# Second feed-forward product of a hybrid decoder layer: seven block products over 1,024 tokens in place of the plain product

## The chip, the cores and the metric

The kernel runs on one core of one Trainium2 chip. The metric is the device time of one execution in microseconds (us); lower is better.

## The reference, cut to what matters

One decoder layer is computed for a prompt of 2,048 tokens and for eight single-token samples that share all weights. It has three mixing branches (a state-space model, trailing pooling, cross-attention to 256 memory tokens), then a gated feed-forward layer:

```python
x = x + rmsnorm(merged @ p['w_out'], p['g_mix_post'])
hf = rmsnorm(x, p['g_ffn_pre']) @ p['w_ffn_in']
f = (jax.nn.silu(hf[..., :D_FF]) * hf[..., D_FF:]) @ p['w_ffn_out']
x = x + rmsnorm(f, p['g_ffn_post'])
```

`D_MODEL` is 1,024 and `D_FF` is 2,816, so `w_ffn_out` is 2,816 x 1,024: 22 blocks of 128 rows by 8 blocks of 128 columns. All data is float32.

## The kernel before, in words

Every matrix product keeps float32 accuracy by splitting each operand into a high and a low part (`split`, L170 to L172: ScalarE copies the high part, VectorE or GpSimd subtracts it to get the low part) and doing three matmuls, high x high, high x low, low x high. Tokens lie along the free axis. The 2,048 prompt tokens are four quarters of 512 (`q` 0 to 3); the eight samples ride along with quarters 0 and 1, four each, which makes their width 516 (`fwidth`). Two quarters make a half (`SB`: quarters 0 and 1, quarters 2 and 3).

**Stages.** Up to about 1,690 us of the span come the branches and the out-projection, quarter by quarter. Then the first feed-forward product, half by half (`ffn_in`, L1309; its pool of buffers is called `half`); then the second (`ffn_out`, L1383; pool `down`), quarter by quarter.

**First feed-forward stage.** For each half, `left` (L1298) loads 28 operand tiles (seven sums by four row blocks) from DRAM (`d_S`) through the four `xr` buffers and splits them into the `S` tiles. The 22 iterations of `ffn_in` each do seven block products with them (a Strassen-Winograd scheme over two quarters and two halves of the 1,024 rows, with 7 products instead of 8), in 7 x 24 = 168 matmuls of 258 or 256 columns. Each iteration needs a pair of weight blocks: `w_pair` (L262) loads two 512 KB tiles into the `wr` buffers (L258), forms four sums on VectorE (L265 to L268) and splits. `prefetch` emits the pair of iteration i+1 at the start of iteration i. At its end the iteration stores the two results, one for each quarter, to `d_f` (L1368). Three times in each iteration `step()` runs the next piece of the background work; during the first half that is `second_scale` (1 piece) and `sums(1)` (16 pieces), which make the second half's `d_S`. What is left of it is run by `flush()` after the 22nd iteration.

**Second feed-forward stage.** For each quarter, `load_f` (L1371) loads 22 tiles of `d_f` through `xr` and splits them into the `f` tiles (52 buffers). `ffn_out` does, for each of 8 output blocks, 22 x 3 matmuls in two column blocks (258 or 256 columns). Weights come in 24 pieces for each pass, 120 in all, because the last quarter is done in two halves of 256 columns with the weights loaded twice. ScalarE takes the result out of PSUM, once squared and once times the gain; `finish` (L1407) normalises, adds the residual and stores.

**What sets the order.** The Python code allocates named buffers from rings: `xr` has 4 buffers, `wr` 4, `wh` and `wl` 4, `tmp` 7. A scheduler places the instructions on each engine's queue, and may move them far ahead of their place in the program when their data and buffers are there. All loads and stores are issued from the SP queue, in its order. The following lines are the parts the steps refer to most:

```python
BUFS = {"U": 5, "G": 2, "ops": 6, "h": 16, "br": 24, "acc": 8, "rb2": 1,
        "xr": 4, "tmp": 7, "rb": 1, "wr": 4, "wh": 4, "wl": 4, "wt": 2,
        "ev": 4, "S": 56, "f": 52, "z": 8}
def w_load(key):
    raw = slot("wr")
    nc.sync.dma_start(raw, I["w_all"][_WIDX[key]])
    return raw
def flush():
    step(1 << 30)
```

Of the kernel before, what the change touches and what calls it, by code (L numbers as in the profile page):

```python
# [29 lines left out]
NB = BW // P  # L30
DFF = 2816
NF = DFF // P
FCH = (8, 8, 6)
FOFF = (0, 8, 16)
SB = ((0, 1), (2, 3))
KH = KD // 2
HW_ = TQ + NS // 2
# [19 lines left out]
def _weight_plan():  # L57
    us = [("us", i) for i in range(4)]
    glu = [("gl", i) for i in range(2)]
    proj = [("uq", 0), ("uq", 1), ("KT",), ("V",), ("uq", 2), ("uq", 3)]  # L60
    proj += [("up", 3), ("up", 2), ("up", 1), ("pw",), ("up", 0)]

    def gates(b, ahead):
        r = []
        for j in range(KD):
            if j % 2 == 0:
                r.append(("ub", b, j // 2))
            r.append(("gt", b, j))
        return [r[1], r[2], r[0]] + r[3:] if ahead else r

    wo = [("wo", m) for m in range(KD)]
    fo = [("fo", c, m) for m in range(KD) for c in range(len(FCH))]
    seq = [("wk", h) for h in range(NH)] + [("wv", i) for i in range(4)] + us
    for q in range(NQ):
        seq += proj
        for i, b in enumerate(ORDER[q]):
            if b == 0:
                seq += glu
            seq += gates(b, i != 1)
        seq += wo + us if q + 1 < NQ else wo  # L80
    for sb in range(len(SB)):
        seq += [("f1", f) for f in range(NF)]
    for q in range(NQ):
        seq += fo
    seq += fo
    return seq


_SEQ = _weight_plan()
_STORED = [k for k in dict.fromkeys(_SEQ) if k[0] not in ("KT", "V", "f1")]  # L90
_STORED += [(k, f) for f in range(NF) for k in ("fa", "fb")]
_WIDX = {k: i for i, k in enumerate(_STORED)}


def _ncols(key):
    if key[0] == "pw":
        return NB * P
    if key[0] == "fo":
        return FCH[key[1]] * P
    return KD * P  # L100


# [26 lines left out]
def trunk(ctx, tc, nc, I, O):  # L129
# [8 lines left out]
    SIZE = {"tmp": 528, "ops": 512, "G": 512, "wr": 1024, "wh": 1024, "wl": 1024, "wt": 1024,  # L138
            "ev": HW_, "S": HW_, "f": HW_, "z": HW_}
    COMMON = ("xr", "tmp", "rb", "rb2", "wr", "wh", "wl")  # L140
    stage = [None]

# [21 lines left out]
    def dram(shape, name):  # L164
        return drp.tile(shape, F32, tag=name, name=name, bufs=1)
# [41 lines left out]
    d_rb2 = dram([NQ, P, W520], "d_rb2")  # L207
    d_S = dram([len(SB), 7, KH, P, HW_], "d_S")
    d_f = dram([NQ, NF, P, HW_], "d_f")

    background = []
    queue = {"last": None, "open": True}
# [64 lines left out]
    def w_emit(i):  # L277
        key = seq[i]
        if key[0] == "f1":
            wstate["buf"][i] = w_pair(key[1])  # L280
            return
        n = _ncols(key)
        raw = slot("wr")
        if key[0] == "KT":
            src = d_kt
        elif key[0] == "V":
            src = d_v
        else:
# [1082 lines left out]
    def load_f(q, n):  # L1371
        ft = []
        for f_ in range(NF):
            raw = slot("xr")
            nc.sync.dma_start(raw[:, :n], d_f[q, f_, :, :n])
            hi, lo = slot("f", F32R), slot("f", F32R)
            split(hi[:, :n], lo[:, :n], raw[:, :n])
            ft.append((hi, lo))
        return ft

    def ffn_out(ft, bl, z, st):
        sl = slice(bl[0][0], bl[-1][0] + bl[-1][1])
        for m in range(KD):  # L1383
            ps = [psum() for _ in bl]
            for c in range(len(FCH)):
                hi, lo = wget("fo", c, m)
                for j in range(FCH[c]):
                    i = FOFF[c] + j
                    ws = slice(j * P, (j + 1) * P)
                    ah, al = ft[i]  # L1390
                    for p_, (o, nn) in zip(ps, bl):
                        T.matmul(p_[:, :nn], lhsT=hi[:, ws], rhs=ah[:, o:o + nn], start=i == 0, stop=False)
                        T.matmul(p_[:, :nn], lhsT=hi[:, ws], rhs=al[:, o:o + nn], start=False, stop=False)
                    for p_, (o, nn) in zip(ps, bl):
                        T.matmul(p_[:, :nn], lhsT=lo[:, ws], rhs=ah[:, o:o + nn], start=False, stop=i == NF - 1)
            if len(z) <= m:
                z.append(slot("z"))
            sq = st if m == 0 else slot("tmp")
            for p_, (o, nn) in zip(ps, bl):
                zs = slice(o, o + nn)  # L1400
                S.activation(sq[:, zs], p_[:, :nn], AF.Square)
                S.activation(z[m][:, zs], p_[:, :nn], AF.Copy, scale=g_fpost[:, m:m + 1])
            if m > 0:
                V.tensor_tensor(st[:, sl], st[:, sl], sq[:, sl], ADD)
            step()

    def finish(q, z, st, bl):  # L1407
        sl = slice(bl[0][0], bl[-1][0] + bl[-1][1])
        if q + 1 == NQ:
            rb = spread(rsqrt_rows(st, bl), 0)[:, :sl.stop - sl.start]  # L1410
        else:
            rb = slot("rb")
            rsqrt_quick(rb, st, bl)
            rb = rb[:, sl]
        yield
        e = min(sl.stop, TQ)
        for k in range(KD):
            xt = slot("xr")
            load_half(xt, d_x2[:, k], q)
            zk = z[k][:, sl]  # L1420
            V.tensor_tensor(zk, zk, rb, MUL)
# [100 lines left out]
    stage[0] = down.__enter__()  # L1522
    slot("z")
    for q in range(NQ):
        n = fwidth(q)
        ft = load_f(q, n)
        z = []
        st = slot("tmp")
        for bl in ([[(0, n // 2), (n // 2, n // 2)]] if q + 1 < NQ else [[x] for x in HALVES]):
            ffn_out(ft, bl, z, st)  # L1530
            flush()
            background.append(finish(q, z, st, bl))
    flush()
    down.__exit__(None, None, None)

# [7 lines left out]
def _pack(a):  # L1543
# [8 lines left out]
    for key, i in _WIDX.items():  # L1552
# [11 lines left out]
        elif kind == "pw":  # L1564
            v = a["pool_w"][0].transpose(1, 0, 2).reshape(P, -1)
        elif kind == "gl":
            v = np.concatenate([kt(a["ssm_w_glu"][0][:, m * P:(m + 1) * P]) for m in (2 * key[1], 2 * key[1] + 1)], axis=1)
        elif kind == "ub":
            w = a["w_branch_up"][0][key[1]]
            v = np.concatenate([kt(w[:, m * P:(m + 1) * P]) for m in (2 * key[2], 2 * key[2] + 1)], axis=1)  # L1570
        elif kind == "gt":
            o = 3 * BW + key[1] * DM + key[2] * P
            v = kt(w_in[:, o:o + P])
        elif kind == "wo":
            v = kt(a["w_out"][0][:, key[1] * P:(key[1] + 1) * P])
        elif kind == "fa":
            v = kt(a["w_ffn_in"][0][:, key[1] * P:(key[1] + 1) * P])
        elif kind == "fb":
            v = kt(a["w_ffn_in"][0][:, DFF + key[1] * P:DFF + (key[1] + 1) * P])
        else:  # L1580
            o = FOFF[key[1]] * P
            v = kt(a["w_ffn_out"][0][o:o + FCH[key[1]] * P, key[2] * P:(key[2] + 1) * P])
# [51 lines left out]
```

## Time and profile before

| What | Value |
|---|---|
| Time, median of 3 runs (lowest to highest) | 3139.98 us (3139.03 to 3144.41) |
| The profiled execution's own time | 3146.45 us |
| Its span, first to last instruction | 3144.5 us |
| TensorE matmul busy, share of the span | 2996.9 us, 95% |
| VectorE busy | 1858.3 us, 59% |
| ScalarE busy | 1214.7 us, 39% |
| GpSimd busy | 741.6 us, 24% |
| First feed-forward stage, from its first matmul to its last | 1696.5 to 2598.3 us |
| Second feed-forward stage, from its first matmul to the end | 2599.9 to 3144.5 us |

TensorE is the engine that is nearly always at work, so a stage is read by how many matmuls it has, how long one takes when nothing holds it up, and where the count falls short. Busy time of TensorE overlaps itself (matmuls are pipelined), so counts over a window, and not busy shares, give the real rate.

### The profile page before, as it was taken

The page shows a single profiled execution, that of the slowest core. Times are in us where ns is not written, and L with a number is a line of the kernel's source. Part 1 is how long each engine was busy: PE and PEld are TensorE (multiplying, and loading weights), DVE is VectorE, ACT ScalarE, POOL GpSimd, SP SyncE. Part 2 cuts the span into 40 slices and gives each one's busy share as a digit, 9 for nine tenths or more (in the row PEclk, how much of TensorE's full clock was granted, in tenths as well). Part 3 has the DMA queues.
Part 4 walks back from the last instruction along what each step waited for, and adds up shares of the span by engine and source line. Part 5 has one row for each costly group of instructions (what it writes and reads, how often), then busy time and mean ns, then how long its engine had stood idle before and what let it go on. Part 6 is the DMA issues. An engine that isn't in the chain of part 4 may idle for free.

```text
span 3144.5 us, 51655 instructions
## 1 busy us (share of the span) xinstructions
PE 2996.9 (95%) x20479; PEld 2764.9 (88%) x20479; DVE 1858.3 (59%) x3187; ACT 1214.7 (39%) x2105; POOL 741.6 (24%) x630
## 2 busy tenths in 40 slices
PE   7989998799999999999996999999999999999997
PEld 6778877689997888878885999999999998999997
DVE  7777756664538644585566855557555554445364
ACT  4532434322445333452333433335333334334343
POOL 2565244532245122440222000000000000011012
PEclk8989999899999999999997999999999999999999
DMA  6344333662334433354364732225222225445475
GB/s 210 112 161 138 120 121 116 163 218 91 127 121 149 137 102 127 120 174 133 110 219 143 233 114 76 78 77 175 81 81 81 81 84 176 153 153 170 159 253 171
DMA packets 205730, 433.02 MB, mean 138 GB/s; under 512 B 47472, under 2 KB 55216, under 8 KB 205488
## 3 DMA queue, kind: packets, MB, share of 16 engines
q1 hardware_dynamic: 205488, 429.72, 43.1%
q8 instruction: 160, 2.62, 0.4%
q14 instruction: 82, 0.67, 0.1%
HBM read 362.82 MB, written 66.49 MB: 137 GB/s over the span
## 4 chain that ended last, share of the span: by engine, by line
PE 82%; DVE 5%; DMA 5%; issue 3%; POOL 2%; ACT 2%; SPq 1%; DVEq 0%; POOLq 0%; ACTq 0%
PE pa L117 78%; PE pb L117 3%; DMA xr<-d_f 1%; DVE wl L172 1%; PE pb L120 1%; DMA xr<-in_ck 1%; DMA xr<-d_S 1%; DVE acc L1238 1%; DMA xr<-in_cv_t 0%; ACT wh L171 0%; SPq L679 0%; DMA ops<-d_ops 0%; POOL acc L1239 0%; DMA xr<-d_qs 0%; DVE G L815 0%
## 5 line engine op out<-in xcount | busy, mean ns | idle before, releaser
L117 PE MATMUL pa<-S,wh 128*128 128x258 f32 (+1 forms) x4928 | 887.4, 283 | 26.1 <-ACT S L171 20.1
L171 ACT ACTIVATE wh<-wr 128x1024 fp32r<-128x1024 f32 (+1 forms) x460 | 458.2, 996 | 1022.4 <-PE pa L117 744.1
L117 PEld LDWEIGHTS pa<-S,wh 128*128 128x128 f32 x4928 | 762.5, 190 | 29.4 <-ACT S L171 21.4
L117 PE MATMUL pa<-S,wl 128*128 128x258 f32 (+1 forms) x2464 | 693.6, 282 | 0.3 <-DVE wl L172 0.3
L117 PE MATMUL pa<-h,wh 128*128 128x512 f32 (+2 forms) x2560 | 667.2, 356 | 19.5 <-ACT tmp L1037 7.4
L172 DVE TENSOR_TENSOR wl<-wr,wh 128x1024 fp32r<-128x1024 f32 x372 | 434.2, 1169 | 393.5 <-ACT wh L171 380.8
L117 PEld LDWEIGHTS pa<-h,wh 128*128 128x128 f32 x2560 | 438.4, 192 | 86.5 <-ACT tmp L1037 7.6
L117 PE MATMUL pa<-br,wh 128*128 128x512 f32 (+2 forms) x1848 | 471.3, 351 | 15.0 <-ACT wh L171 8.8
L117 PE MATMUL pa<-f,wh 128*128 128x258 f32 (+1 forms) x2816 | 468.9, 283 | 5.9 <-DVE f L172 3.0
L117 PEld LDWEIGHTS pa<-S,wl 128*128 128x128 f32 x2464 | 465.6, 189 | 0.5 <-DVE wl L172 0.5
L117 PE MATMUL pa<-h,wl 128*128 128x512 f32 (+2 forms) x1280 | 420.7, 355 | 0.0
L117 PEld LDWEIGHTS pa<-f,wh 128*128 128x128 f32 x2816 | 400.1, 190 | 8.4 <-DVE f L172 4.3
L117 PEld LDWEIGHTS pa<-br,wh 128*128 128x128 f32 x1848 | 311.6, 190 | 62.8 <-ACT wh L171 8.8
L172 POOL TENSOR_TENSOR wl<-wr,wh 128x1024 fp32r<-128x1024 f32 (+1 forms) x88 | 214.2, 2436 | 442.2 <-ACT wh L171 392.5
L117 PE MATMUL pa<-f,wl 128*128 128x258 f32 (+1 forms) x1408 | 312.3, 283 | 4.5 <-DVE wl L172 4.5
L117 PE MATMUL pa<-br,wl 128*128 128x512 f32 (+2 forms) x924 | 295.4, 350 | 1.0 <-DVE wl L172 1.0
L117 PEld LDWEIGHTS pa<-h,wl 128*128 128x128 f32 x1280 | 231.4, 192 | 33.6
L1365 POOL TENSOR_TENSOR tmp<-tmp,ev 128x516 f32<-128x516 f32 (+1 forms) x44 | 59.9, 1362 | 841.2 <-ACT tmp L1364 820.9
L172 DVE TENSOR_TENSOR wl<-wt,wh 128x1024 fp32r<-128x1024 f32 x88 | 108.1, 1228 | 223.5 <-ACT wh L171 223.5
L117 PEld LDWEIGHTS pa<-f,wl 128*128 128x128 f32 x1408 | 229.8, 189 | 4.7 <-DVE wl L172 4.7
L117 PEld LDWEIGHTS pa<-br,wl 128*128 128x128 f32 x924 | 164.1, 190 | 24.3 <-DVE wl L172 1.4
L1339 ACT ACTIVATE ev<-pa 128x258 f32<-128x258 f32 (+1 forms) x264 | 101.0, 385 | 196.7 <-PE pa L117 166.8
(329 smaller groups left out, 3486.7 us busy)
## 6 DMA issues: line engine op xcount, KB each, us to landing
wr<-in_w_all SPq DMA_DIRECT2D x408, 512.0 KB, 3.5
ops<-d_ops SPq DMA_DIRECT2D x112, 256.0 KB, 3.6
xr<-in_x_t SPq DMA_DIRECT2D x80, 256.0 KB, 3.7
xr<-d_x SPq DMA_DIRECT2D x72, 256.0 KB, 4.1
wr<-in_w_all SPq DMA_DIRECT2D x40, 384.0 KB, 3.4
d_f<-tmp SPq DMA_DIRECT2D x44, 258.0 KB, 4.7
xr<-d_f SPq DMA_DIRECT2D x44, 258.0 KB, 3.7
d_f<-tmp SPq DMA_DIRECT2D x44, 256.0 KB, 4.3
```

The lines of the kernel that those rows point to most:

```text
L117: self._done(self.nc.tensor.matmul(*a, **k))
L120: self._done(self.nc.tensor.transpose(*a, **k))
L171: S.activation(dst_hi, src, AF.Copy)
L172: (eng or V).tensor_tensor(dst_lo, src, f(dst_hi), SUB)
L1238: V.tensor_tensor(zk, zk, rb[:, :n], MUL)
L1339: both(lambda u, s: S.activation(dst[:, s], X[u][:, :w], AF.Copy))
L1365: G.tensor_tensor(f0[:, :n], f0[:, :n], p1[:, :n], MUL)
```

## The change

The second product becomes seven block products too, over a half (two quarters, 1,024 tokens) at a time: rows of `f` in two blocks of 11 x 128 (`KF` = 11), columns of `w_ffn_out` in two blocks of 4 x 128. Seven products (in the order `OUT_ORDER`), each 4 output blocks by 11 row blocks by 3 matmuls, replace the eight that the plain product would be.

- The left operand's four sums are made in the first stage by `out_sums`: for each of 11 row pairs, four loads of `d_f` into `xr`, four GpSimd operations, four stores to the new `d_fs`. `ffn_in` walks its 22 blocks in the order 0, 11, 1, 12, ... (`FORD`), and queues the pair before last as background work at every second iteration; the last pair is queued after the loop and run by `flush()`.
- The weights' four sums are made by `out_weights`, six background pieces queued behind `sums(1)` in the first half: for each, four 512 KB loads into `wr`, four GpSimd operations, four stores to the new `d_T`.
- In the second stage, `load_f` loads 11 tiles for each of the 14 products (one product ahead; 44 `f` buffers), from `d_f` or `d_fs`. Weights come in six pieces for each product; with the last product of the second half done in two halves of 256 columns, 90 pieces. The second half's other products use one column block of 512. VectorE adds each product to its running sums out of PSUM; ScalarE squares, GpSimd (VectorE at the very end) adds the squares.
- In the last `finish`, the residual tiles are loaded once into `z` buffers instead of twice into `xr`.

```diff
-            "ev": 4, "S": 56, "f": 52, "z": 8}
+            "ev": 4, "S": 56, "f": 44, "z": 16, "st": 3}
...
-        split(hi[:, :n], lo[:, :n], raw[:, :n], G if key[0] in ON_POOL or i >= len(seq) - KD else V)
+        split(hi[:, :n], lo[:, :n], raw[:, :n], G if key[0] in ON_POOL or i >= len(seq) - len(FPC) else V)
...
-        for f_ in range(NF):
+        for at, f_ in enumerate(FORD):
...
+            if at % 2 and at > 1:
+                background.append(out_sums(sb, at // 2 - 1))
             step()
+        background.append(out_sums(sb, KF - 1))
+
+    def out_sums(sb, j):
+        n = fwidth(SB[sb][0])
+        A = []
+        for q in SB[sb]:
+            for f_ in (j, j + KF):
+                t = slot("xr")
+                nc.sync.dma_start(t[:, :n], d_f[q, f_, :, :n])
+                A.append(t[:, :n])
+        a11, a12, a21, a22 = A
+        G.tensor_tensor(a22, a21, a22, ADD)
+        G.tensor_tensor(a21, a11, a21, SUB)
+        G.tensor_tensor(a11, a22, a11, SUB)
+        G.tensor_tensor(a12, a12, a11, SUB)
+        for i, t in enumerate((a22, a11, a21, a12)):
+            nc.sync.dma_start(d_fs[sb, i, j, :, :n], t)
+        yield
+
+    def out_weights():
+        for c in range(len(FPC)):
+            n = FPC[c] * P
+            b11, b12, b21, b22 = (w_load(("fo", r, m, c))[:, :n] for r in range(2) for m in range(2))
+            G.tensor_tensor(b22, b22, b12, SUB)
+            G.tensor_tensor(b12, b12, b11, SUB)
+            G.tensor_tensor(b11, b11, b22, ADD)
+            G.tensor_tensor(b21, b21, b11, SUB)
+            for i, t in enumerate((b21, b12, b11, b22)):
+                nc.sync.dma_start(d_T[i, c, :, :n], t)
+            yield
...
+        for m in range(KH):
             ps = [psum() for _ in bl]
+            for k in range(KF):
+                c, j = divmod(m * KF + k, 8)
+                if j == 0:
+                    wpiece[0] = wget("w2", i, c)
...
+            elif i == 1:
+                c11.append(slot("z"))
+                plus(c11[m], u[m], ps)
+                squares(0, c11[m])
...
+            for _ in range(3):
+                next(loader, None)
             step()
...
         if sb + 1 < len(SB):
             background.append(second_scale(NQ - 1))
             background.append(sums(sb + 1))
+            background.append(out_weights())
         ffn_in(sb, got)
         flush()
...
+    plan = [(sb, i) for sb in range(len(SB)) for i in OUT_ORDER]
+    ft = []
+    run(load_f(*plan[0], ft))
+    for at, (sb, i) in enumerate(plan):
...
+        loader = load_f(*plan[at + 1], nxt) if at + 1 < len(plan) else iter(())
+        for bl in out_halves(sb, i):
+            ffn_out(sb, i, ft, bl, C, st, loader)
```

## Rows read from the trace of the kernel before

**Rows 1.** The page: busy time of TensorE, and the chain that ended last.

```profile
PE 2996.9 (95%) x20479; PEld 2764.9 (88%) x20479; DVE 1858.3 (59%) x3187; ACT 1214.7 (39%) x2105; POOL 741.6 (24%) x630
...
PE 82%; DVE 5%; DMA 5%; issue 3%; POOL 2%; ACT 2%; SPq 1%; DVEq 0%; POOLq 0%; ACTq 0%
```

**Rows 2.** Stretches, with counts: window, length, PE, PEld, DVE, ACT, POOL, PEclk, DMA share, GB/s.

```profile
1690.00:1745.00 55.00, 38.85 (x257) 36.42 (x258) 46.58 (x79) 29.77 (x53) 6.93 (x5) 0.80 0.76 235
...
2165.00:2190.00 25.00, 24.28 (x197) 23.44 (x196) 19.68 (x33) 14.51 (x27) 1.30 (x1) 1.00 0.70 212
2190.00:2598.00 408.00, 408.00 (x3446) 408.00 (x3445) 219.56 (x367) 149.98 (x268) 27.16 (x21) 1.00 0.28 83
2598.00:2640.00 42.00, 36.23 (x266) 33.91 (x266) 26.07 (x37) 22.46 (x37) 0.00 (x0) 0.96 0.78 240
2640.00:3000.00 360.00, 360.00 (x3025) 360.00 (x3024) 156.29 (x202) 134.62 (x226) 24.82 (x16) 1.00 0.49 159
```

**Rows 3.** A stream of 512-column matmuls, earlier stage: start, us; 27 such `wl` rows.

```profile
1540.27 0.40 PE L117 MATMUL pa<-br,wl 128*128 128x512 f32 x1
...
1558.38 0.39 PE L117 MATMUL pa<-br,wl 128*128 128x512 f32 x1
```

**Rows 4.** SP queue, first feed-forward stage: weight loads of two iterations.

```profile
1901.61 0.33 SPq L258 DMA_DIRECT2D wr<-in_w_all  x1
...
1905.29 0.33 SPq L258 DMA_DIRECT2D wr<-in_w_all  x1
...
1921.70 0.47 SPq L258 DMA_DIRECT2D wr<-in_w_all  x1
```

**Rows 5.** SP queue, quarter 1: loads into the `xr` buffers.

```profile
506.56 0.43 SPq L382 DMA_DIRECT2D xr<-in_x_t  x1
...
556.43 0.37 SPq L1084 DMA_DIRECT2D xr<-d_qs  x1
556.86 0.97 SPq L1088 DMA_DIRECT2D xr<-in_ck  x2
...
696.65 0.63 SPq L382 DMA_DIRECT2D xr<-in_x_t  x1
```

**Rows 6.** Weight splits and GpSimd operations, 2300 to 3145 us: busy, mean ns, idle before.

```profile
L172 DVE TENSOR_TENSOR wl<-wr,wh 128x1024 fp32r<-128x1024 f32 x89 | 111.1, 1248 | 138.5 <-ACT wh L171 138.4
L171 ACT ACTIVATE wh<-wr 128x1024 fp32r<-128x1024 f32 x94 | 99.6, 1060 | 197.0 <-PE pa L117 183.5 <-DMA wr<-in_w_all 6.3 <-issue 4.6
...
L1365 POOL TENSOR_TENSOR tmp<-tmp,ev 128x512 f32<-128x512 f32 x15 | 19.4, 1293 | 277.7 <-ACT tmp L1364 277.7
...
L172 POOL TENSOR_TENSOR wl<-wr,wh 128x1024 fp32r<-128x1024 f32 x5 | 12.0, 2399 | 11.8 <-ACT wh L171 11.8
```

**Rows 7.** Time to landing: weight pairs (min/median/max), then stores and loads (median).

```profile
DMA to landing us min/median/max: 3.1/4.2/6.8
...
d_f<-tmp SPq DMA_DIRECT2D x44, 256.0 KB, 4.3
xr<-d_f SPq DMA_DIRECT2D x44, 256.0 KB, 4.2
```

**Rows 8.** The end of the first stage: last matmul, and the two last stores.

```profile
2598.05 0.28 PE L117 MATMUL pa<-S,wl 128*128 128x256 f32 x1
...
2600.02 0.33 SPq L1368 DMA_DIRECT2D d_f<-tmp  x1
...
2601.75 0.33 SPq L1368 DMA_DIRECT2D d_f<-tmp  x1
```

**Rows 9.** VectorE in the tail, waiting for residual tiles.

```profile
3138.32 0.43 DVE L1422 TENSOR_TENSOR z<-z,xr 128x256 f32<-128x256 f32 x1 [3.34 <-DMA xr<-d_x]
3141.43 0.43 DVE L1422 TENSOR_TENSOR z<-z,xr 128x256 f32<-128x256 f32 x1 [2.69 <-DMA xr<-d_x]
```

**Rows 10.** Two stretches in which GpSimd and VectorE are both busy.

```profile
2760.00:2770.00 10.00, 10.00 (x85) 10.00 (x85) 9.46 (x8) 2.95 (x6) 8.54 (x5) 1.00 0.46 145
3020.00:3030.00 10.00, 5.75 (x49) 5.54 (x48) 10.00 (x6) 4.80 (x8) 9.15 (x6) 1.00 0.57 180
```

More of the change, by code (lines that the diff above doesn't have):

```diff
@@ L32 @@
 NF = DFF // P
-FCH = (8, 8, 6)
-FOFF = (0, 8, 16)
+KF = NF // 2
+NPC = 4 * KF
+FPC = tuple(min(8, NPC - c) for c in range(0, NPC, 8))
+FORD = tuple(x for j in range(KF) for x in (j, j + KF))
+OUT_ORDER = (0, 1, 5, 4, 6, 2, 3)
+OUT_BLOCK = {0: (0, 0), 1: (1, 0), 2: (1, 1)}
+OUT_SUM = {4: 0, 5: 1, 6: 2, 2: 3}
 SB = ((0, 1), (2, 3))
@@ L81, in _weight_plan, with out_halves @@
     for sb in range(len(SB)):
[L82 to L85, printed above, removed]
-    return seq
+        seq += [("f1", f) for f in FORD]
+    for sb in range(len(SB)):
+        for i in OUT_ORDER:
+            seq += [("w2", i, c) for c in range(len(FPC))] * len(out_halves(sb, i))
+    return seq
+def out_halves(sb, i):
+    if sb == 0:
+        return [[(0, HW_ // 2), (HW_ // 2, HW_ // 2)]]
+    return [[(0, TQ // 2)], [(TQ // 2, TQ // 2)]] if i == OUT_ORDER[-1] else [[(0, TQ)]]
 _SEQ = _weight_plan()
-_STORED = [k for k in dict.fromkeys(_SEQ) if k[0] not in ("KT", "V", "f1")]
+_STORED = [k for k in dict.fromkeys(_SEQ) if k[0] not in ("KT", "V", "f1", "w2")]
 _STORED += [(k, f) for f in range(NF) for k in ("fa", "fb")]
+_STORED += [("fo", r, n, c) for c in range(len(FPC)) for r in range(2) for n in range(2)]
 _WIDX = {k: i for i, k in enumerate(_STORED)}
@@ L209, in trunk @@
     d_f = dram([NQ, NF, P, HW_], "d_f")
+    d_fs = dram([len(SB), 4, KF, P, HW_], "d_fs")
+    d_T = dram([4, len(FPC), P, KD * P], "d_T")
     background = []
@@ L287, in w_emit @@
             src = d_v
+        elif key[0] == "w2":
+            src = d_T[key[1] - 3, key[2]] if key[1] > 2 else I["w_all"][_WIDX[("fo",) + OUT_BLOCK[key[1]] + key[2:]]]
         else:
@@ L1374, in load_f @@
+    def load_f(sb, i, out):
+        n = fwidth(SB[sb][0])
+        for k in range(KF):
+            if i in OUT_SUM:
+                src = d_fs[sb, OUT_SUM[i], k]
+            else:
+                src = d_f[SB[sb][i // 2], k + KF * (i > 0)]
             raw = slot("xr")
-            nc.sync.dma_start(raw[:, :n], d_f[q, f_, :, :n])
+            nc.sync.dma_start(raw[:, :n], src[:, :n])
             hi, lo = slot("f", F32R), slot("f", F32R)
             split(hi[:, :n], lo[:, :n], raw[:, :n])
-            ft.append((hi, lo))
@@ L1379, in load_f, with ffn_out @@
-        return ft
-    def ffn_out(ft, bl, z, st):
+            out.append((hi, lo))
+            yield
+    def ffn_out(sb, i, ft, bl, C, st, loader):
+        u, c11, c12, c22 = C
         sl = slice(bl[0][0], bl[-1][0] + bl[-1][1])
-        for m in range(KD):
-            ps = [psum() for _ in bl]
[L1385 to L1404, printed above, removed]
@@ new lines, in plus, with squares @@
+        def plus(dst, src, ps):
+            for p_, (o, nn) in zip(ps, bl):
+                V.tensor_tensor(dst[:, o:o + nn], src[:, o:o + nn], p_[:, :nn], ADD)
+        def squares(row, t):
+            if st[row] is None:
+                st[row] = slot("st")
+                S.activation(st[row][:, :fwidth(SB[sb][0])], t[:, :fwidth(SB[sb][0])], AF.Square)
+                return
+            sq = slot("tmp")
+            S.activation(sq[:, sl], t[:, sl], AF.Square)
+            (G if sb == 0 or i != 3 else V).tensor_tensor(st[row][:, sl], st[row][:, sl], sq[:, sl], ADD)
@@ new lines, in ffn_out @@
+        for m in range(KH):
+            ps = [psum() for _ in bl]
+            for k in range(KF):
+                c, j = divmod(m * KF + k, 8)
+                if j == 0:
+                    wpiece[0] = wget("w2", i, c)
+                hi, lo = wpiece[0]
+                ws = slice(j * P, (j + 1) * P)
+                ah, al = ft[k]
+                for p_, (o, nn) in zip(ps, bl):
+                    T.matmul(p_[:, :nn], lhsT=hi[:, ws], rhs=ah[:, o:o + nn], start=k == 0, stop=False)
+                    T.matmul(p_[:, :nn], lhsT=hi[:, ws], rhs=al[:, o:o + nn], start=False, stop=False)
+                for p_, (o, nn) in zip(ps, bl):
+                    T.matmul(p_[:, :nn], lhsT=lo[:, ws], rhs=ah[:, o:o + nn], start=False, stop=k == KF - 1)
+            if i == 0:
+                u.append(slot("z"))
+                for p_, (o, nn) in zip(ps, bl):
+                    S.activation(u[m][:, o:o + nn], p_[:, :nn], AF.Copy)
+            elif i == 1:
+                c11.append(slot("z"))
+                plus(c11[m], u[m], ps)
+                squares(0, c11[m])
+            elif i == 5:
+                plus(u[m], u[m], ps)
+            elif i == 4:
+                c12.append(slot("z"))
+                plus(c12[m], u[m], ps)
+            elif i == 6:
+                c22.append(slot("z"))
+                plus(c22[m], c12[m], ps)
+                plus(u[m], u[m], ps)
+                squares(1, c22[m])
+            elif i == 2:
+                plus(c12[m], c12[m], ps)
+                squares(0, c12[m])
+            else:
+                plus(u[m], u[m], ps)
+                squares(1, u[m])
+            for _ in range(3):
+                next(loader, None)
@@ L1405, in ffn_out @@
             step()
+    wpiece = [None]
+    last_x = []
     def finish(q, z, st, bl):
@@ L1417, in finish @@
         for k in range(KD):
-            xt = slot("xr")
-            load_half(xt, d_x2[:, k], q)
+            if q + 1 < NQ:
+                xt = slot("xr")
+                load_half(xt, d_x2[:, k], q)
+            elif len(last_x) > k:
+                xt = last_x[k]
+            else:
+                xt = slot("z")
+                last_x.append(xt)
+                load_half(xt, d_x2[:, k], q)
             zk = z[k][:, sl]
-            V.tensor_tensor(zk, zk, rb, MUL)
+            V.scalar_tensor_tensor(zk, zk, g_fpost[:, k:k + 1], rb, MUL, MUL)
             (V if q + 1 == NQ and k % 2 else G).tensor_tensor(zk, zk, xt[:, sl], ADD)
@@ L1522, in trunk @@
     stage[0] = down.__enter__()
[L1523 to L1532, printed above, removed]
+    for tag in ("f", "z", "st"):
+        slot(tag)
+    plan = [(sb, i) for sb in range(len(SB)) for i in OUT_ORDER]
+    ft = []
+    run(load_f(*plan[0], ft))
+    for at, (sb, i) in enumerate(plan):
+        if i == OUT_ORDER[0]:
+            C, st = ([], [], [], []), [None, None]
+        nxt = []
+        loader = load_f(*plan[at + 1], nxt) if at + 1 < len(plan) else iter(())
+        for bl in out_halves(sb, i):
+            ffn_out(sb, i, ft, bl, C, st, loader)
+            if i == 2:
+                background.append(finish(SB[sb][0], C[1] + C[2], st[0], bl))
+            elif i == 3:
+                flush()
+                background.append(finish(SB[sb][1], C[0] + C[3], st[1], bl))
+        run(loader)
+        ft = nxt
     flush()
@@ L1580, in _pack @@
         else:
-            o = FOFF[key[1]] * P
-            v = kt(a["w_ffn_out"][0][o:o + FCH[key[1]] * P, key[2] * P:(key[2] + 1) * P])
+            _, r, n, c0 = key
+            v = []
+            for t in range(8 * c0, 8 * c0 + FPC[c0]):
+                m, k = n * KH + t // KF, r * KF + t % KF
+                v.append(a["w_ffn_out"][0][k * P:(k + 1) * P, m * P:(m + 1) * P])
+            v = np.concatenate(v, axis=1)
         w_all[i, :, :v.shape[1]] = v
```

10 lines of the change are left out of this document (3 added, 7 removed).

## The prediction

> **What bounds the kernel now.** I read the page first: TensorE is busy 95% of the span and makes up 82% of the chain that ended last [rows 1]. So a stage is worth what its matmuls take, plus the places where they wait. The stretches give both [rows 2]. In the second feed-forward stage 360 us hold 3,025 matmuls: 119.0 ns each, with nothing lost. From 2190 to 2598, the first stage's second half, it is 408 / 3,446 = 118.4 ns, again without loss. The short rows show the ramps: in the 42 us after 2598 there are 266 matmuls, 31.7 us of work, so 10.3 us are lost; in the 25 us after 2165, where the second half begins, 197, so 1.6 are lost; in the 55 us after 1690, where the first half's 28 operand tiles are loaded through four `xr` buffers, 257, so 24 are lost. The question for the change is whether it takes out more matmul time than it adds waits in front of TensorE. So next I read who holds the small buffer rings.
>
> **A 512-column matmul.** 27 `wl` rows lie 18.11 us apart from first to last, so 26 triples, 0.697 us each, 232.2 ns a matmul [rows 3]: 2 ns less than two narrow ones. The Trainium skill, page "TensorE: Matmul & The Clock Gate", section "Back-to-back issue gap", gives a sustained 131 ns at 512 columns, by which 792 of them would take an estimated 80 us less; the trace of this kernel does not agree, and its 232 ns decides.
>
> **The change, part by part** (sum against the profiled execution's 3146.45 us, 6.5 above the median 3139.98).
>
> *Matmuls.* Before: 4 quarters x 8 x 22 x 3 x 2 = 4,224 at 119.0 ns = 502.7 us. After: first half 7 x 4 x 11 x 3 x 2 = 1,848 narrow ones; second half 6 x 132 = 792 of 512 columns and 264 narrow ones. 2,112 x 119.0 ns + 792 x 232.2 ns = 435.2 us. **Gain 67 us.**
>
> *Splits, sums and evictions of the second stage.* 154 operand splits instead of 88, 90 weight splits instead of 120, sums out of PSUM on VectorE. VectorE is busy 43% and ScalarE 37% of the 360 us stretch [rows 2]; they stay under TensorE, and I cost them at nothing. If that cover went, the 66 extra splits at some 1.3 us would be the price. The loads, about 82 MB for 79, fit as well.
>
> *Weight sums, in the `wr` ring.* Buffers seem to be given out in program order. In quarter 1 the last load of one piece of work goes out at 506.56. The next `xr` user in the program must wait for a store to `d_qs` and loads at 556.43; the loads of `in_ck` and `in_x_t` behind it need only inputs, yet they come at 556.86 and 696.65 [rows 5]. A later user does not pass an earlier one. Now `out_weights` takes all four `wr` buffers for each of its pieces c0 to c5. `second_scale` and `sums(1)` take 17 steps and an iteration has three, so c0 falls in iteration 5, c1 to c3 in iteration 6, c4 and c5 in iteration 7. Weight pair 7 is emitted before c1, pair 8 after c3, pair 9 after c5.
> One round is a load of 4.2 us, four GpSimd operations at 2.40, a store of 4.3 and some 0.8 for issue and hand-offs: 18.9 us [rows 6, 7]. The operand of the first operation is the fourth tile loaded, and each store must land before its buffer passes on, so rounds do not overlap. Let t be the start of iteration 6; an iteration lasts 20.1 us and its first weight load goes out just after it begins [rows 4]. c0 gets its last buffer at t + 1.5; pair 7 follows in time, its second tile free again at t + 26.3. c1, c2, c3 take until t + 83.0, with the first buffer free 7.5 earlier; pair 8 then needs a load (4.5 with issue) and a split (2.4): t + 82.4. Iteration 8 was due at t + 40.2: a **wait of 42 us**. For pair 9: 6.5 us into iteration 8 c4 can start, 18.9, then c5 (half as wide) frees its first buffer after 10.3, then 6.9: 42.6 us against 20.1, a **wait of 22.5 us**. Together 65. Bounds: landings at the least and most seen (3.1, 6.8 us [rows 7]) make a round 17 to 24 us, and the sum, about four rounds less 10, 58 to 86. I take the median. Behind the waiting split nothing else feeds TensorE: all six PSUM banks belong to the iteration.
>
> *Operand sums at the end of each half.* `flush()` emits the last `out_sums` in front of the next stage's loads, in the same four `xr` buffers. It needs the last iteration's stores. Those go out 3.4 us after the last matmul's end, T = 2598.3 [rows 8]; landing T + 7.7; load 4.2 and issue: T + 12.3; the first of four operations at 1.29: T + 13.6; its store lands at T + 18.0 [rows 6, 7]. Only then does the next load go out. Now those loads go out ahead of the end.
> At the start of the second half: 18 us, then the 24 us ramp of 28 loads as at 1690, less the 1.6 lost today [rows 2]: **40 us**. Bounds: 30, if SP and DMA are less loaded than at 1690; 48, if stores land as late as 6.8.
> At the start of the second stage: load and split of the first tile, T + 24.0, in place of a start at T + 1.6; the ramp after it as today: **22 us** (15 to 28).
>
> *Clock.* Where TensorE waited at 1690 the granted clock averages 0.80 of 2.4 GHz, and 0.96 after 2598 [rows 2]: parts of these stretches ran at 1.2 GHz. In the ramps that is included; after the two weight waits I add **4 us** (0 to 10).
>
> *Other work added to the first stage.* GpSimd: 88 operations at 1.29 and 24 for the weights, 167 us in 860, beside 58 now; DMA some 69 MB, so 81 GB/s becomes about 160, below the 235 of the ramps; SP some 220 issues at 0.33 us. Hidden by TensorE; price if not, below.
>
> *Tail.* The last residual tiles are loaded ahead; VectorE's waits of 3.34 and 2.69 us [rows 9] go, and one sum out of PSUM joins the end: **5 us less** (3 to 8).
>
> Sum: -67 + 65 + 40 + 22 + 4 - 5 = **+59**, 3205 us on the profiled execution, 3199 against the median. With all bounds the same way 3170 to 3245.
>
> **The rivals.**
> *Faster: the weight loads do not queue behind the sums.* If pairs 8 and 9 get their buffers before c1 to c5, the 65 and 4 go: -10, 3130 us. It decides in the `wr` ring in iterations 6 to 8, and from a wait of 5 us downwards the change is not slower: a round of under 4 us, less than its load. So only the order can do it, not faster rounds. For it: most pairs are loaded nearly two iterations ahead. Against it: rows 5, and that the sums' loads need nothing but inputs, so a scheduler that goes by readiness would take them first as well.
> *Faster by more: neither ring holds anything up.* Then the matmuls and the tail are the whole, 3140 - 72 = 3068 us. For it: today the next stages' first loads go out ahead of the stage's end. Against it: no earlier user of `xr` is left then.
> *Slower still: GpSimd shuts VectorE out.* From 3020 to 3030 GpSimd is busy 9.15 us, VectorE all the time, and TensorE does 49 matmuls of some 84: 4.2 us lost. From 2760 to 2770 GpSimd is busy 8.54 and TensorE loses nothing [rows 10]. 167 us of new GpSimd work would cost 0 by the one and 77 by the other. In the first stage a weight split has a whole iteration's time, which is nearer to the second row, so the forecast takes 0; half of 77 gives 3238 us. The Trainium skill, page "SBUF — State Buffer", section "Who interferes with whom", says that a VectorE instruction with two SBUF inputs and a GpSimd one that reads SBUF exclude each other for the whole instruction; the trace agrees that both lengthen, and does not say what TensorE loses by it here.
>
> **How the numbers follow.** The forecast's case gets 0.62, the first rival 0.14, the second 0.10, the third 0.08; 0.06 is for what I have not seen. A difference of 0.2%, 6 us, is about what a measurement of this kernel can tell from none. Faster: the second rival, most of the first and a part of the unseen, 0.23. The same: the edge of the first, 0.07. Slower: 0.70. The likeliest case's own range is 3170 to 3245; to hold 8 in 10 the range takes in the first rival with its bounds, from 3118, and most of the third, to 3240.
>
> **What would show it right or wrong.** Right: two gaps of some 40 and 20 us on TensorE in iterations 8 and 9 of the first half (between about 1870 and 1980 us), ended by weight splits that waited for `wr` loads, with `d_T` stores just before; a gap of 18 to 25 us at each stage's start with GpSimd working on `xr`; the second stage's matmul stretch near 435 us plus ramps. Wrong: weight loads in an unbroken 20 us beat while `d_T` is stored, or `d_S` and `d_f` loads that go out before the last `d_fs` stores. If the gaps are there and the time is still lower, the term on the matmuls was too small.

## The result, and the profile after

Four runs of the changed kernel have their median at 3213.36 us (3210.96 to 3214.76), four of the kernel before at 3142.19 us: a ratio of 1.0223, 95% interval 1.0210 to 1.0236, so 2.2% slower. The prediction was 3199 us and slower. By the medians the change costs 71 us. The profiled execution's span is 3211.1 us against 3144.5, so in the traces 66.6 us are to be found.

The page of the kernel after, busy times and the chain that ended last:

```profile
PE 2938.1 (91%) x19159; PEld 2670.6 (83%) x19159; DVE 1952.2 (61%) x3286; ACT 1206.2 (38%) x2061; POOL 969.7 (30%) x764
...
PE 34%; DMA 3%; DVE 2%; POOL 1%; issue 0%; ACT 0%; SPq 0%; POOLq 0%; DVEq 0%; ACTq 0%
```

TensorE is busy 59 us less than in [rows 1], and its share of the span falls from 95% to 91%: the work went down and the waiting went up. The chain's shares add up to only some two fifths, because this chain could be followed back no further than about 1885 us; they are not to be set beside those of [rows 1]. So the stretches again, columns as in [rows 2]:

```profile
1800.00:1900.00 100.00, 76.43 (x618) 75.71 (x616) 46.15 (x67) 23.83 (x46) 44.66 (x25) 0.90 0.72 237
1900.00:2000.00 100.00, 42.34 (x318) 42.13 (x319) 25.95 (x39) 15.83 (x28) 38.44 (x21) 0.68 0.61 202
...
2200.00:2300.00 100.00, 73.94 (x565) 71.27 (x564) 52.69 (x83) 39.54 (x71) 15.94 (x11) 0.88 0.53 162
2300.00:2700.00 400.00, 400.00 (x3378) 400.00 (x3378) 237.13 (x367) 147.77 (x265) 93.86 (x61) 1.00 0.44 133
2714.00:2756.00 42.00, 19.71 (x150) 19.29 (x149) 16.86 (x24) 13.52 (x23) 5.05 (x4) 0.76 0.68 211
2756.00:2956.00 200.00, 200.00 (x1671) 200.00 (x1670) 123.07 (x184) 87.59 (x130) 25.43 (x16) 1.00 0.61 194
...
3170.00:3180.00 10.00, 2.95 (x25) 2.75 (x24) 10.00 (x6) 0.44 (x1) 10.00 (x6) 0.81 0.84 262
3180.00:3190.00 10.00, 7.53 (x48) 7.56 (x49) 9.30 (x20) 1.69 (x4) 7.35 (x5) 0.68 0.45 133
```

An unbroken 100 us of the first half holds 838 matmuls of 119.3 ns. From 1800 to 2000 us there are 618 + 318 = 936, so 740 are missing: **88 us**, the lower granted clock (0.90 and 0.68 of 2.4 GHz on average, so in part 1.2 GHz) included. Of the 844 that 100 us hold in the second half, 565 are done from 2200 to 2300: **33 us**, where 1.6 were lost before. In the 42 us after the first stage's last matmul there are 150: **24 us** lost, 10.3 before [rows 2]. After 3170 us it is some 11 us in 20.

What TensorE waited for, 1800 to 2000 us (the view of waits: in total, times, longest; then, from the timeline, TensorE's three waits one by one, in the last bracket):

```profile
PE pa L128 <- ACT wh L182: 81.1, 3, 53.6
ACT wh L182 <- DMA wr<-in_w_all: 80.8, 3, 53.5
POOL wr L1410 <- DMA wr<-in_w_all: 50.7, 5, 15.8
```

```profile
1860.61 2.09 PE L128 MATMUL pa<-S,wh 128*128 128x258 f32 x8 [6.83 <-ACT wh L182]
...
1937.00 2.09 PE L128 MATMUL pa<-S,wh 128*128 128x258 f32 x8 [53.62 <-ACT wh L182]
...
1979.60 2.09 PE L128 MATMUL pa<-S,wh 128*128 128x258 f32 x8 [20.66 <-ACT wh L182]
```

TensorE waits for the split of a new weight pair, and the split for the pair's load. Why the load is late stands in the chain of waits before the longest of them (start, us, what):

```profile
1911.02 2.35 POOL wr L1413
...
1913.39 4.64 DMA d_T<-wr
...
1918.05 4.48 DMA wr<-in_w_all
...
1922.72 2.31 POOL wr L1410
...
1925.10 2.34 POOL wr L1411
...
1927.53 2.34 POOL wr L1412
...
1929.89 0.32 SPq L1415
...
1930.26 5.55 DMA wr<-in_w_all
...
1935.89 1.07 ACT wh L182
```

This is one round as the prediction drew it: the sum's store lands, the next piece's load takes the buffer, GpSimd works, the stores go out, and only then the weight pair is loaded. The chain alone does not tell the ring from SP's queue: the pair's load goes out directly behind SP's issue of a store (L1415). From 1800 to 2000 us SP waits 26.1 us before weight loads (L271) for a store to `d_T` to land, and 44 us at L1415 for GpSimd's sums. Runs 1 and 6 separate the two. The ends of the stages look as drawn too. SP's queue at the start of the second stage:

```profile
2717.57 0.93 SPq L1383 DMA_DIRECT2D d_f<-tmp  x2
2723.85 1.27 SPq L1395 DMA_DIRECT2D xr<-d_f  x3
2729.70 3.00 SPq L1403 DMA_DIRECT2D d_fs<-xr  x3
2732.76 1.13 SPq L1426 DMA_DIRECT2D xr<-d_f  x2
```

The last matmul of the first stage begins at 2713.99; the first of the second at 2736.34, after 22.1 us of waiting. Between lie the stores of the last iteration, the operand sums' loads and stores, and only then the stage's own loads (L1426).

### The profile page after: what moved, and what is told of

Its sections match the earlier page's. It is cut to its first block, busy times and chain, and to the rows that moved or that the text cites. A ratio compares the mean times of both kernels' runs of the same rounds, so it can differ in the third digit from the quotient of the medians.

```text
span 3211.1 us, 49759 instructions
## 1 busy us (share of the span) xinstructions
PE 2938.1 (91%) x19159; PEld 2670.6 (83%) x19159; DVE 1952.2 (61%) x3286; ACT 1206.2 (38%) x2061; POOL 969.7 (30%) x764
## 5 line engine op out<-in xcount | busy, mean ns | idle before, releaser
L128 PE MATMUL pa<-S,wh 128*128 128x258 f32 (+1 forms) x4928 | 898.4, 285 | 135.1 <-ACT wh L182 81.1
L182 ACT ACTIVATE wh<-wr 128x1024 fp32r<-128x1024 f32 (+1 forms) x430 | 428.1, 996 | 931.5 <-PE pa L128 586.6
L183 DVE TENSOR_TENSOR wl<-wr,wh 128x1024 fp32r<-128x1024 f32 x344 | 406.8, 1183 | 314.2 <-ACT wh L182 301.1
L128 PE MATMUL pa<-f,wh 128*128 128x258 f32 (+2 forms) x1936 | 398.8, 315 | 22.3 <-ACT f L182 22.1
L183 POOL TENSOR_TENSOR wl<-wr,wh 128x1024 fp32r<-128x1024 f32 x86 | 211.5, 2462 | 435.2 <-ACT wh L182 385.4
L128 PEld LDWEIGHTS pa<-f,wh 128*128 128x128 f32 x1936 | 298.3, 191 | 45.8 <-ACT f L182 22.3
L128 PE MATMUL pa<-f,wl 128*128 128x258 f32 (+2 forms) x968 | 253.5, 314 | 0.0
L1380 POOL TENSOR_TENSOR tmp<-tmp,ev 128x516 f32<-128x516 f32 (+1 forms) x44 | 70.0, 1591 | 427.9 <-ACT tmp L1379 427.9
L128 PEld LDWEIGHTS pa<-f,wl 128*128 128x128 f32 x968 | 161.9, 189 | 11.5
```

The source lines that it names most:

```text
L128: self._done(self.nc.tensor.matmul(*a, **k))
L182: S.activation(dst_hi, src, AF.Copy)
L183: (eng or V).tensor_tensor(dst_lo, src, f(dst_hi), SUB)
L1380: G.tensor_tensor(f0[:, :n], f0[:, :n], p1[:, :n], MUL)
```

## The experiments

**1 to 4: each suspected wait taken away, and no sums at all.** The first moves the weight sums into the `xr` ring:

```diff
-            b11, b12, b21, b22 = (w_load(("fo", r, m, c))[:, :n] for r in range(2) for m in range(2))
+            for o in range(0, FPC[c] * P, 4 * P):
...
+                        t = slot("xr")
+                        nc.sync.dma_start(t[:, :4 * P], I["w_all"][_WIDX[("fo", r, m, c)]][:, o:o + 4 * P])
```

> The weight sums (same GpSimd operations in number of elements, same bytes, same place in the order) use the xr ring in pieces of 512 columns, so no weight pair has to pass a wr buffer held by a sum. Ring theory (the 88 us lost between 1850 and 1980 us are waits for wr buffers): all weight pairs come in their beat, the three gaps go, 3213 - 88 = 3125 us, between 3115 and 3140, since operand tiles of that stretch need xr only at stage starts. Contention theory (the loss comes from 24 long GpSimd operations and 44 MB of DMA beside the splits, whatever the ring): the work is all still there, so 3190 us or more. If the xr ring is held just as badly at the stage starts, the start of the second half waits longer than 31 us, and the gain shrinks by that.

Measured: 3159.32 us, 54 less than the changed kernel; against the kernel before 1.0045 (1.0027 to 1.0062). Most of the 88 us go, with the same bytes and elements; the waits for weight splits are gone. (The bytes are some 23 MB by the loads and stores in the code, not the 44 of the expectation.) The edit also halves the pieces, eleven rounds in place of six, and no run has half pieces in the `wr` ring; that the ring itself holds the loads up is told by run 6. But 310 matmuls are still missing between 1850 and 2100 us, 37 us, and no longer for weight splits (waits of VectorE, 1840 to 2070 us, and of TensorE):

```profile
DVE wt L278 <- DMA wr<-in_w_all: 40.6, 7, 12.0
...
PE pa L128 <- DVE ev L1357: 21.4, 8, 7.8
```

The second takes the last operand sums behind the loads of the stage that follows:

```diff
-        background.append(out_sums(sb, KF - 1))
...
             got = left(sb)
+        if sb:
+            background.append(out_sums(sb - 1, KF - 1))
...
     run(load_f(*plan[0], ft))
+    run(out_sums(len(SB) - 1, KF - 1))
```

> Only the last operand sums of each half move: they are issued after the loads of the stage that follows. Hand-off theory: the gap of 22 us at the start of the second stage and some 31 us at the start of the second half go, all but the 1.6 us ramp of the kernel before and perhaps 10 us of ramp after 2714 us as there, so 3213 - 31 - 20 = about 3162 us, between 3155 and 3175; the weight gaps of 88 us stay as they are. Ramp theory (the loads of the next stage are slow in any case, because stores, loads and sums share the DMA engines): the first loads come earlier but the tiles still trickle in, 3200 us or more.

Measured: 3169.88 us, 43 less; 1.0080 (1.0065 to 1.0095). TensorE's first matmul of the second stage waits 1.60 us instead of 22.07, and 2200 to 2300 us holds 804 matmuls instead of 565; the weight waits stay (80.1 us in three). So the place of the last sums is the cause of the two waits at the hand-offs.

```profile
2683.87 1.01 PE L128 MATMUL pa<-f,wh 128*128 128x258 f32 x6 [1.60 <-ACT f L182]
...
2200.00:2300.00 100.00, 97.88 (x804) 95.99 (x803) 75.15 (x117) 48.34 (x89) 19.32 (x13) 1.00 0.66 204
```

The third has both edits.

> Both edits together. If the two losses are separate, as the sum of the prediction takes them, the gains add: 3213 - 88 - 51 = about 3074 us, between 3062 and 3090, and faster than the kernel before (3142). If GpSimd or the DMA engines were the common cause, 3160 us or more.

Measured: 3120.32 us, 0.9922 (0.9904 to 0.9940): faster than the kernel before. The gains add (54 + 43 = 97, measured 93), but 46 us short of the expectation's 3074. The fourth tells whether that is the sums:

```diff
-            if i in OUT_SUM:
-                src = d_fs[sb, OUT_SUM[i], k]
...
+            src = d_f[SB[sb][i // 2 % 2], k + KF * (i > 0)]
...
-            background.append(out_weights())
```

> Leaves out all sums of operands and weights: the seven block products take plain operand tiles and plain weights in their places, so the output is another, while matmuls, splits, sums out of PSUM and the loads of the second stage stay. It measures the term on the matmuls without any cost of the sums. By that term: 3142 - 67 - 5 = about 3070 us, between 3060 and 3080. If the second stage itself had grown dearer (ramps, VectorE in its last product), 3085 us or more; a result under 3060 would say that the matmul term was too small. Against the run with both edits it gives what the sums still cost once no ring is in the way: 0 to 15 us.

Measured: 3076.29 us, 0.9787 (0.9772 to 0.9802): 68 us under the kernel before. This is the change without the cost of its sums; the sums as the change has them cost 3213 - 3076 = 137 us, and with both edits still 44, where the expectation had 0 to 15. Where those sit is told by the chain of waits of the third run, 1985 to 2045 us:

```profile
2003.80 2.59 DMA d_fs<-xr
...
2006.41 0.32 SPq L1394
...
2006.78 4.90 DMA wr<-in_w_all
...
2011.80 1.66 DVE wt L278
2013.46 0.35 DVE ev L1357
```

Two queues stand here one behind the other. SP waits at L1394 for a buffer whose store has not landed; the weight load queued behind it needs nothing of that, but goes out only then (from 1850 to 2060 us SP's waits in front of weight loads themselves add up to under 2 us). VectorE waits at L278 for these weights, and the eviction (L1357) behind it, which frees TensorE's PSUM bank, waits too. The Trainium skill, page "DMA: Bandwidth & Descriptors", section "Anatomy of one DMA — SWDGE (gpsimd) path", says that a DMA's semaphore wait happens on the issuing sequencer before dispatch. It says so in a section on DMAs that GpSimd issues; the row on L1394 shows the same on SP.

**5 to 7: SP's queue.** The loads and stores of both kinds of sums are issued by GpSimd, in the kernel with both edits and in the changed kernel; beside them, in the kernel with both edits, the last product's weight splits go to VectorE.

```diff
-                nc.sync.dma_start(t[:, :n], d_f[q, f_, :, :n])
+                nc.gpsimd.dma_start(t[:, :n], d_f[q, f_, :, :n])
...
-            nc.sync.dma_start(d_fs[sb, i, j, :, :n], t)
+            nc.gpsimd.dma_start(d_fs[sb, i, j, :, :n], t)
```

> As the run with both edits (3120 us), but all loads and stores of the sums are issued by GpSimd, not by SP. In that run TensorE still loses some 34 us between 1850 and 2060 us: SP stands for 143 us in that stretch in front of stores of sums (the sum is not done) and 66 us in front of loads into buffers whose store has not landed, the weight loads stand behind it, and VectorE, waiting for them, evicts late. Queue theory: with the sums out of SP's queue this goes, 3120 - 34 = about 3086 us, between 3078 and 3095. Contention theory (what is left is DMA and SBUF load): 3112 us or more. GpSimd then waits for its own loads, and the weight splits and additions that it has in the same stretch come later: if these feed TensorE in time no loss, else 3110 us or more, with waits of TensorE for splits on GpSimd.

Measured: 3158.25 us, 1.0057 (1.0042 to 1.0072): slower than with SP, a miss in the sum, though not in the place. (The 143 and 66 us of the expectation are those of 1780 to 2160 us; from 1850 to 2060 they are 104 and 38.) Two stretches of this run, then what ended the longest waits from 2140 to 2260 us:

```profile
1800.00:2150.00 350.00, 350.00 (x2928) 350.00 (x2927) 258.83 (x320) 127.00 (x227) 195.73 (x224) 1.00 0.57 187
2150.00:2250.00 100.00, 35.34 (x224) 31.79 (x223) 33.05 (x48) 24.17 (x43) 38.29 (x48) 0.66 0.57 182
```

```profile
ACT S L182 <- DMA xr<-d_S: 71.4, 16, 57.6
...
PE pa L128 <- ACT S L182: 61.3, 5, 58.9
```

From 1800 to 2150 us, with every weight sum and 196 us of GpSimd's time in it, some 77 of them for issuing DMAs, TensorE loses nothing: the 34 us go with the sums out of SP's queue, and the work beside it costs nothing. The sums' 69.40 MB now also run on a DMA queue of their own (q0, software_dynamic on the page), so issuing order and transport changed together. But the rounds, about 20 us each (the load waits for the round before to land), pile up behind each other, and the operand tiles of the second half wait 58 us for `xr` buffers: SP stands 45.4 us in front of one of their loads (L1318) until a store to `d_fs` lands.

> The changed kernel (3213 us) with the loads and stores of the sums issued by GpSimd; the wr ring and the place of the last sums stay. It tells the ring from SP's queue as the cause of the 88 us of weight waits: if the queue were the cause, they go as far as in the run before this one, 3213 - 88 = about 3125 us plus what the hand-offs hold. If the ring is (weight pairs 7, 8 and 9 need buffers that the sums hold until their stores land), the loads of weights still wait for these buffers: 60 us or more of the 88 stay, 3185 us or more. Splits on GpSimd behind the sums may add to it.

Measured: 3250.25 us, 1.0352 (1.0337 to 1.0368). With SP's queue freed and the ring kept, TensorE waits 107 us in three for weight splits in the first half, instead of 81 in three. SP's own waits there (1800 to 2100 us: in total, times, longest):

```profile
SPq L271 <- DMA d_T<-wr: 68.3, 6, 52.9
```

No sum stands on SP's queue any more, and its weight loads still wait up to 52.9 us for a store out of a `wr` buffer. So the ring is a cause by itself. GpSimd now issues, waits and works in one queue, and the waits are longer for it; which of its waits lengthens them was not separated.

> As the run with both edits (3120 us), but the weight splits of the last product are on VectorE, not on GpSimd. Before the last matmuls of the stage TensorE waits 11.7 us for a sum of squares on VectorE, which stands behind eight scalings that take 15.3 us beside GpSimd's splits and additions. If GpSimd's splits are what stretches them: six splits of about 1.2 us more on VectorE, the eight scalings at some 0.7 to 1.2 us, so 3 to 10 us less, 3110 to 3117 us. If the additions on GpSimd alone do it: no gain, 3118 to 3126 us.

Measured: 3113.50 us, 0.9923 (0.9906 to 0.9939). The time lies in the range of a gain, but the ratio to the kernel before, measured beside it, is the same as without the edit (0.9922), so no gain is shown. The eight scalings fall from 15.3 to 11.6 us, VectorE takes the splits instead, and TensorE then waits 5.2 us for those and 4.1 for the squares in place of 11.7.

**8 and 9: half the weight sums in the second half.** Three of the six pieces stay, three are queued in the second half, with the sums on GpSimd's queue and on SP's:

```diff
-    def out_weights():
-        for c in range(len(FPC)):
+    def out_weights(part):
+        for c in range(3 * part, 3 * part + 3):
```

> As the run with both edits and the sums' loads and stores on GpSimd's queue (3158 us), but only six of the eleven pieces of weight sums stand in the first half, the other five in the second. In that run nothing is lost from 1800 to 2150 us, but the rounds of some 21 us run late into the start of the second half, where the loads of its operand tiles wait up to 58 us for xr buffers. Backlog theory: eleven rounds of weight sums and ten of operand sums do not fit between 1800 and 2160 us one after another; with five weight rounds (some 105 us) moved, the loads come in time, 3158 - 61 = about 3097 us, between 3085 and 3108, since 16 rounds of the second half fit in its 410 us. Rival: GpSimd's queue orders the last operand sums of the first half against the loads in the same way however few rounds stand before, 3140 us or more.

Measured: 3096.44 us, 0.9853 (0.9837 to 0.9870): 1.5% faster than the kernel before, and the best but for a variant of it below. The first half runs full from 1800 to 2100 us (2,511 matmuls in 300 us). It still lies 20 us above the run without sums. 12 of them stand where the second half begins, 738 matmuls from 2100 to 2200 us against 837 there.

> The same split of the weight sums between the halves, but with all loads and stores issued by SP (as in the run with both edits, 3120 us). If SP's queue blocks once per round (some 35 us of TensorE's time over eleven rounds of weight sums), moving five rounds to the second half moves their losses along: 3112 to 3126 us. If what blocks is only the density of sums in six iterations (weights and operands at once), the loss shrinks to less than half: 3095 to 3105 us.

Measured: 3113.95 us, 0.9908 (0.9892 to 0.9923). The losses move along with the sums: 153 matmuls short from 1850 to 2000 us, 95 short from 2200 to 2350 (25 in the run without the split), together 30 us. Without the split it was 34 us from 1850 to 2100. So moving the rounds does not free TensorE while SP issues them; against run 8, which differs in the issuing queue alone, it is 17.5 us slower.

**10: the round without its arithmetic**, the changed kernel with the four GpSimd lines of `out_weights` taken out.

> The changed kernel (3213 us) without the four GpSimd operations on each piece of weights: the tiles are loaded into wr and stored unchanged, so the sums of weights are left out and the output is another; all loads, stores, buffers and orders stay. It prices the round. By the prediction's working a round falls from 18.9 to 9.3 us, the wait before pair 8 from 42 to 13 and before pair 9 from 22.5 to 8, so 44 us less: 3169 us, and down to 3150 if the measured 88 us shrink in proportion. If the loss does not hang on the round's length (the bytes beside the weight loads, or SP's queue), 3195 us or more.

Measured: 3151.51 us, 1.0038 (1.0023 to 1.0052), 62 us less, the lower end that the expectation named. From 1800 to 2000 us 1,427 matmuls of 1,676 are done: 30 us lost where it was 88, two waits (25.7 us) where it was three. The loss hangs on the length of the round, GpSimd's operations and their place in its queue included, and not on the bytes alone.

**11: the tail**, on the eighth kernel, `step(2 if i == 3 else 1)` at the end of `ffn_out`.

> The run with the sums on GpSimd's queue and split between the halves (3096 us), with two steps of background work instead of one after each row of the last product, so that the eight scalings and additions of the quarter before are spread over that product's first half instead of standing together at its end (there TensorE waits some 11 us for VectorE). If their bunching is the cause: 4 to 10 us less, 3086 to 3093 us. If it is the exclusion between VectorE and GpSimd itself, the same work takes as long wherever it stands: 3094 to 3100 us.

Measured: 3094.02 us, 0.9852 (0.9830 to 0.9874), not to be told from 0.9853. The wait of TensorE at the end is the same 11.8 us to the tenth. But the edit did not do what it was made for: `finish` runs its eight scalings in one piece between two `yield`s, so a second step cannot spread them, and they stand together as before (VectorE, run 8, then this run):

```profile
3043.70 15.34 DVE L1520 SCALAR_TENSOR_TENSOR z<-z,gv,rb 128x512 f32<-128x512 f32 x8
3040.85 15.35 DVE L1520 SCALAR_TENSOR_TENSOR z<-z,gv,rb 128x512 f32<-128x512 f32 x8
```

So whether their bunching is the cause stays untested.

## Why the prediction was right

The direction and the mechanism stand; the steps, in its order:

- **Matmuls, -67: right.** From 2995 to 3135 us 605 matmuls of 512 columns in 140 us are 231 ns each, against 232.2 from [rows 3] (6 ns less than two narrow ones, not 2; the sum does not use the difference). From the stage's first matmul to its last it is 458 us after and 526 before, 68 less, each some 23 above its count. Without the sums the change gives 68 us; the prediction's matmuls and tail together said 72.
- **Weight sums, +65 and +4 for the clock: right in kind, too small.** It lost 88. The waits were 6.8, 53.6 and 20.7 us where 0, 42 and 22.5 were drawn. The round itself was right: the last stores of the pieces went out at 1858.0, 1887.7, 1913.4, 1932.3, 1957.9 and 1974.3, and where nothing came between, 1913.4 to 1932.3, it is 18.9 us, as worked out. One thing missed is that the round shares GpSimd's queue with `out_sums`. In the round before the undisturbed one, GpSimd waits 12.46 us for an operand tile and then does the two in turn (timeline of GpSimd):

```profile
1898.97 1.27 POOL L1398 TENSOR_TENSOR xr<-xr,xr 128x516 f32<-128x516 f32 x1 [12.46 <-DMA xr<-d_f]
...
1901.55 2.34 POOL L1410 TENSOR_TENSOR wr<-wr,wr 128x1024 f32<-128x1024 f32 x1
1903.85 1.27 POOL L1400 TENSOR_TENSOR xr<-xr,xr 128x516 f32<-128x516 f32 x1
1905.07 2.34 POOL L1411 TENSOR_TENSOR wr<-wr,wr 128x1024 f32<-128x1024 f32 x1
```

So that round takes 25.7 us, 6.8 more than drawn, where the wait for pair 8 came out 11.6 us longer. The round before, behind weight pair 7, takes 29.7; the 6.8 us that pair 7 itself waited were not followed. The upper bound on the round, 24, was made from DMA times alone and did not hold.
- **Operand sums, +40 and +22: right in kind, too large.** The second half's start lost 33 us, 31 more than before, near the lower bound of 30. At the second stage the wait is 22.1, but its price is 24 - 10.3 = 14, just under the lower bound of 15: "the ramp after it as today" was the error, since after 2736 us the matmuls run nearly full; the loads had caught up while TensorE stood. With the sums moved the two hand-offs gave back 43.
- **Tail, -5: off.** From the last matmul to the end it is 16.6 us against 18.2, 2 less. In front of it TensorE waits 11.7 us for the squares on VectorE, behind eight scalings of 1.99 us beside GpSimd's splits and additions (groups, 3160 to 3186 us):

```profile
L1515 DVE SCALAR_TENSOR_TENSOR z<-z,gv,rb 128x512 f32<-128x512 f32 x8 | 15.3, 1986 | 0.0
...
L183 POOL TENSOR_TENSOR wl<-wr,wh 128x1024 fp32r<-128x1024 f32 x5 | 12.8, 2577 | 7.7 <-ACT wh L182 7.7
...
L1516 POOL TENSOR_TENSOR z<-z,xr 128x512 f32<-128x512 f32 x7 | 11.3, 1628 | 0.6 <-DVE z L1515 0.6
```

"Splits, sums and evictions at nothing" fails here: the last 264 matmuls take 45.7 us where their count gives 31.4. [rows 10] had shown 4.2 us lost in the same place. The other 2,640 of the stage are 9 us above their count, the ramp after 2736 us included.
- **Other work in the first stage, nothing: right for GpSimd and DMA, incomplete for SP.** Run 5 holds all the weight sums from 1800 to 2150 us without loss, and run 8 six of their eleven pieces from 1800 to 2100, so the rival "GpSimd shuts VectorE out" is out in this stage; in run 5 VectorE is busy 259 of the 350 us and has room. SP's issues were counted (220 at 0.33 us), but not what stands behind a waiting one. In the changed kernel this lies under the longer ring waits; once these are gone it costs 34 us.

The account from the spans: matmuls -67, weight waits +88, half start +31, stage start +14, tail -2, the first stage's first matmul at 1690.3 instead of 1696.5 for -6, and +8 for what is left over (some 3 in the first stage and 5 in the second): +66. The -6 is not explained. In the traces of the kernels with the change the first matmul stands between 1687.3 and 1693.2, so they differ as much among themselves, and for the kernel before there is one trace, of an execution 6.5 us above the median. That the errors nearly cancel (19 too little on the weights, 17 too much on the hand-offs) is luck. (With all bounds one way the prediction's terms add up to 3168 and 3242, not 3170 and 3245; nothing hangs on it.)

Of the rivals, "the weight loads do not queue behind the sums" and "neither ring holds anything up" are out by runs 1, 2 and 6. The second one's 3068 us is what the fourth run nearly reaches, 3076, with the sums gone.

## What to carry to other kernels

What the hidden work cost here was decided by its buffers and its queue, not by the engine's time: ask of each added step which ring it allocates from, whose turn comes next there, and what stands behind its waiting DMA on the issuing queue. A sum that takes all four buffers of a ring through a load, four operations and a store turns the ring into a lock of 19 us a round; moving it to another ring and another queue, spreading it out, and issuing it behind the next stage's loads made of a loss of 2.2% a gain of 1.5%. And when one blockage goes, look for the next: here ring, SP's queue and the backlog of rounds each showed only when the one before was gone.

## What the runs showed that was not expected

- A DMA issued by GpSimd takes 0.54 to 0.58 us of that engine (rows of `xr<-d_f` and `d_fs<-xr` in the run with both edits and its own queue), where SP's takes 0.32 to 0.36 for the same tiles (medians in the run with both edits).
- One late load stops TensorE through two queues, SP's and VectorE's: of the 40 us that VectorE waited for weights at L278 in the third run, 20.9 came through to TensorE as late evictions.
- GpSimd's operation on 1024 columns takes 2.34 us, on 516 columns 1.27: in halves the same work takes 2.54 in place of 2.34, so smaller pieces cost GpSimd little.
- The scalings of 512 columns on VectorE take 1.99 us each beside GpSimd's splits and additions, and 1.51 with the splits on VectorE; the same operation takes 0.74 earlier in the kernel (L453). In their place in the kernel before stands a product of two tiles, 1.50 us beside GpSimd's additions. The Trainium skill, page "SBUF — State Buffer", section "Who interferes with whom", has VectorE's instruction with two SBUF inputs and GpSimd's that reads SBUF exclude each other; the trace agrees in kind. What this costs TensorE was not separated: it waits 11.7 us with GpSimd's splits beside the scalings and 9.3 with these on VectorE (run 7).
